# Adding the residual rows: by a load and a VectorE addition, or by a transfer that accumulates into SBUF

## The chip, the cores and the metric

The kernel runs on one core of a Trainium2 chip. A core has five engines with a queue of instructions each: TensorE (PE, matmuls), VectorE (DVE), ScalarE (ACT), GpSimd (POOL) and SyncE (SP, which here begins nearly all transfers between HBM and the on-chip memory SBUF). An engine works its queue in order; an instruction that has to wait, for a semaphore of another engine or of a transfer, holds everything behind it in that queue. The metric is the device time of one execution in microseconds (us), lower is better.

## What is computed

One decoder layer over 4096 rows of width 1024, in float32. The normalised and modulated input feeds three groups of heads (banded attention, RWKV-7, gated linear attention); their gated outputs are joined, go through one output projection, and the result is normalised, gated and added to the input row:

```python
y = jnp.concatenate([attn, rwkv, gla], axis=-1) @ w_out
return x + gate[:, None] * _rmsnorm(y, g_post)
```

The change concerns the last line only, the addition of `x`.

## The kernel before

The rows are cut into 16 tiles of `NT` = 256 rows (`NS` = 16), and each tile into two halves of 128 rows, one row per SBUF partition. A first part (to about 1075 us) prepares the weights and runs the two recurrent groups over all tiles, writing their outputs to a scratch tensor in HBM (`mscr`). A second part runs attention and the output projection, tile by tile: `stage_s` and `stage_v` belong to attention, `stage_m` joins the groups and splits the joined values into pairs of float16 (`mtp`), and `stage_p2` does, for tile i, the output of tile i - 1 (`outp`), the gates (`gates`, matmuls into `gp`) and the queries, keys and values of the next tile (`qkv`, matmuls into `kp`, `qp`, `vp`; the values go through HBM, `vscr`, and come back as `v` in eight loads).

`outp(i)` computes the projection of the tile as seven products (a fast matrix scheme on halves of the operands) into a PSUM bank `op`. Four of the weight blocks stay in SBUF (`o`), three do not and are loaded in turn into one buffer `ov`, each in two halves, as soon as the product that used the buffer has read a half. DVE and ACT combine the products into `yv`, two buffers of 128 rows x 1024 that all tiles but the last share. When a half is complete, `norm` takes the sum of squares (ACT), forms a reciprocal root in a dozen small DVE steps on one column (`sy`, `nwt`, `ry`), scales the half by it and by the gate row `gn` (the DVE instruction `yv<-yv,ry,x`; `gn` lies in the same buffer as the rows of x, so the profile calls both x), adds the rows of x (`yv<-yv,x`) and has SP store it (`out<-yv`). The rows of x come by SP into `xo`, a single buffer of 128 rows: the second half's rows are loaded as soon as the first addition has read it. The last tile is handled apart (`end`, `last_square`, `last_norm`) with its own buffers.

The order of each engine's instructions is neither that of the program text nor one written by hand. Every call passes through a `Lane`, which gives it to a planner (`Order.note`). The planner estimates the duration of each instruction from its size, notes which one reads or writes what another wrote, and in `pin` plays the whole second part through and fixes, per engine, the order that it found. `rank` is the place in the program's text, moved by `urgent` and `lag`. So an edit of a cost, or a removed instruction, can move others.

Of the kernel before, what the change touches and what calls it, by code (L numbers as in the profile page):

```python
# [12 lines left out]
F32 = mybir.dt.float32  # L13
# [3 lines left out]
ALU = mybir.AluOpType  # L17
# [4 lines left out]
P = 128  # L22
D = 1024
# [40 lines left out]
class Order:  # L64
# [34 lines left out]
    def note(self, eng, name, outs, ins, func, r):  # L99

        st = Step()
        st.ins, st.eng, st.table, st.array, st.bytes, st.then = r.ins, str(eng.engine).split(".")[-1], None, None, 0, []
        st.joint = self.joint
        st.half, st.rank = None, len(self.steps) + self.lag
        e, o = st.eng, outs[0]
        on_psum = [a for a in ins if str(a.tensor.space) == "PSUM"]
        n = max(math.prod(a.shape[1:]) for a in [o, *ins[:1]])
        cols = len([a for a in ins[1:] if math.prod(a.shape[1:]) == 1]) if n > 1 else 0
        if e == "PE":
            f32, lhs = ins[0].dtype == F32, self.region(ins[0])  # L110
            n = math.prod(o.shape[1:])
            _, p0, p1, _ = self.region(o)
            rows, cs = (lhs[1] // 32, (lhs[2] + 31) // 32), (p0 // 32, (p1 + 31) // 32)
            rows, cs = [(0, 4) if b - a > 2 else (a, b) for a, b in (rows, cs)]
            mode = (rows[1] - rows[0], cs[1] - cs[0])
            took = n * (2 if f32 else 1) / 2400 + 0.003
            took = max(took, 0.056 if not f32 else 0.0 if mode[1] < 4 else 0.109 if n > 16 else 0.21)
            issue = 0.017 if f32 and mode == (1, 2) else 0.009 if f32 and mode[0] == 1 else 0.007
            cells = [4 * a + b for a in range(*rows) for b in range(*cs)]
            st.array = (mode, cells, 2 if f32 and name == "matmul" else 1, took, issue)  # L120
            st.occ = st.lat = 0.0
        elif e == "SP":
            st.bytes = math.prod(ins[0].shape) * SIZE[ins[0].dtype]
            kb = st.bytes / 1024
            st.occ = 0.47
            st.lat = next((t for k, t in ((8, 1.9), (32, 2.0), (128, 2.3), (256, 2.6), (512, 3.5)) if kb <= k), 4.8)
        elif e == "Activation":
            st.occ = (0.05 if on_psum else 0.093) + 0.093 * (len(ins) - 1) + 0.832e-3 * n
            st.lat = st.occ + 0.1
            if len(outs) > 1:  # L130
                st.occ += 0.187
                st.lat = st.occ + 0.02
            st.table = LN_TABLE if func == AF.Ln else EXP_TABLE if func in (AF.Exp, AF.Tanh) else None
        elif e == "Pool":
            if name == "memset":
                st.occ = 0.06
            elif name == "tensor_copy":
                st.occ = 0.25 if n <= 2 else 0.11 + 0.95e-3 * n
            else:
                st.occ = 0.42 + 1.5e-3 * n if n <= 512 else 1.85e-3 * n  # L140
            st.lat = st.occ + 0.05
        else:
            if name == "tensor_reduce":
                n = math.prod(ins[0].shape[1:])
            fast = name in ("tensor_scalar", "tensor_single_scalar") and not on_psum and o.dtype == F32
            fixed, rate = 0.065 + 0.06 * (cols > 0), 1.04e-3
            if fast:
                rate = 0.53e-3
            elif name == "transpose":
                fixed = 0.09  # L150
            elif name == "memset":
                fixed, rate = 0.05, 0.3e-3
            elif name == "tensor_tensor" and len(o.shape) == 3 and o.shape[2] <= 16 and n > 16:
                fixed, rate = 0.09, 1.55e-3
            st.occ = fixed + rate * n
            st.lat = st.occ + 0.085

        k, st.needs, st.turn = len(self.steps), {}, []
        out_r, in_r = [self.region(a) for a in outs], [self.region(a) for a in ins]
        if e in ("Activation", "DVE"):  # L160

            st.half = (out_r[0][1], in_r[0][1] if e == "Activation" and in_r and out_r[0][2] - out_r[0][1] <= 64 else None)
        tiles = {a.tensor.name: a.tensor for a in [*outs, *ins]}

        if e == "SP" and self.behind is not None:
            st.turn.append(self.behind)

        def need(j, data=False):
            st.needs[j] = st.needs.get(j, False) or data

        for t, tensor in tiles.items():
            if t not in self.known:
                self.known.add(t)
                if t in self.held and tensor.tag:
                    held = self.slots.setdefault((tensor.owner_uid, tensor.tag), [])

                    if held and self.users.get(held[-1]):
                        st.turn.append(self.users[held[-1]][0])
                    if len(held) == self.held[t]:
                        for j in self.users.get(held.pop(0), ()):  # L180
                            need(j)
                    held.append(t)
            elif t in self.held and self.users.get(t):
                st.turn.append(self.users[t][0])
            if str(tensor.space) == "PSUM":
                for j in self.users.get(t, ()):
                    need(j)

        def meet(a, b):
            return a[1] < b[2] and b[1] < a[2] and (a[3] is None or a[3] & b[3])  # L190

        def covered(a, b):
            return b[1] <= a[1] and a[2] <= b[2] and (a[3] is None or not a[3] & ~b[3])

        for a in in_r:
            for w, j in self.wrote.get(a[0], ()):
                if meet(a, w):
                    need(j, True)
        for a in out_r:
            if a[3] is not None:  # L200
                for old in (self.wrote, self.read):
                    for w, j in old.get(a[0], ()):
                        if meet(a, w):
                            need(j)
                    old[a[0]] = [(w, j) for w, j in old.get(a[0], ()) if not covered(w, a)]
            self.wrote.setdefault(a[0], []).append((a, k))
        for a in in_r:
            self.read.setdefault(a[0], []).append((a, k))
        for t in tiles:
            self.users.setdefault(t, []).append(k)  # L210
        st.needs.pop(k, None)
        self.steps.append(st)
# [108 lines left out]
class Lane:  # L321
# [6 lines left out]
    def __getattr__(self, name):  # L328
        f = getattr(self.eng, name)

        def call(*args, **kw):
# [2 lines left out]
            r = f(*args, **kw)  # L334
            self.model.tc.cur_priority += lift
            aps = [a for a in (*args, *kw.values()) if isinstance(a, bass.AP)]
            outs = [aps[0].tensor.name] + ([kw["accum_out"].tensor.name] if kw.get("accum_out") is not None else [])
            accum = kw.get("accum_out")
            self.model.order.behind = self.model.gate if self.model.stage in ("c", "g") else None
# [59 lines left out]
def hybrid_kernel(ctx, tc, x, rows, ada1, adaw, w1, wl, w2, wo, cst, abias, out):  # L399
# [1497 lines left out]
    def outp(i):  # L1897

        f = F[i]
        x2 = xo if i < NS - 1 else t_hT("xo2").rearrange("p a k n -> p (a k n)").bitcast(F32)  # L1900
        SP.dma_start(x2[:, 0:D], x[i * NT + P : (i + 1) * NT, :])
        yield [("m", i)]
        if i == 0:
            yvs = t_A([P, 2, D], "yv")
# [65 lines left out]
        if end:  # L1970
            last_square(f, 1, 0, sums[1])
            last_norm(f, 1, sums[1], x2[:, 0:D])
            SP.dma_start(x2[:, D : 2 * D], x[i * NT : i * NT + P, :])
        else:
            norm(f["oi"], yv[1], x2[:, 0:D], f["blk"][5].rearrange("p a k n -> p (a k n)"),
                 out[i * NT + P : (i + 1) * NT, :])
            SP.dma_start(x2[:, 0:D], x[i * NT : i * NT + P, :])
        yield from full(6)
        add(y12, y12)
        if end:  # L1980
            last_square(f, 0, 1, sums[0])
            last_norm(f, 0, sums[0], x2[:, D : 2 * D])
        else:
            norm(f["oi"], yv[0], x2[:, 0:D], f["blk"][6].rearrange("p a k n -> p (a k n)"), out[i * NT : i * NT + P, :])
        done.add(("o", i))

    def norm(oi, yv, xt, junk, dst):

        sy = st.tile([P, 1], F32, tag="sy", name="sy")
        S.activation(junk, yv, AF.Square, scale=oi, accum_out=sy)  # L1990
# [2 lines left out]
        rsqrt(ry, sy, 1)  # L1993
        V.tensor_mul(ry, ry, oi)
        V.scalar_tensor_tensor(yv, yv, ry, gn, op0=ALU.mult, op1=ALU.mult)
        V.tensor_add(yv, yv, xt)
        SP.dma_start(dst, yv)

    def stage_p2(i):
# [67 lines left out]
    with tc.If(flag == 0):  # L2067
# [42 lines left out]
        with tc.For_i(0, NS, 1) as iv:  # L2110
# [30 lines left out]
            for a in range(2):  # L2141
                xa, oa = [t[:, a].rearrange("o p d -> (o p) d") for t in rows_of]
                SP.dma_start(xo, xa)
                norm(foi, fyv[a], xo, flat[1][:, 0:D], oa)
            G.tensor_copy(fkT[:, :, :, 0:P], fkT[:, :, :, NT : NT + P])
            G.tensor_copy(fv[0], fv[2])
            G.memset(fpm, 0.0)
# [93 lines left out]
```

## Time and profile before

| | |
|---|---|
| Time, median of 3 runs | 2062.37 us (2061.8 to 2066.6) |
| Profiled execution, first to last instruction (its own time) | 2056.7 us |
| TensorE clock granted, mean | 0.986 |
| PE busy | 1950.2 us (95%) |
| DVE busy | 1590.3 us (77%) |
| ACT busy | 1130.8 us (55%) |
| POOL busy | 220.5 us (11%) |
| Addition `yv<-yv,x` | 30 times 1.224 us |
| Load of 128 rows of x (512 KB), from issue to landing | 30 times, median 4.2 us |
| Store `out<-yv` (512 KB) | 30 times, median 2.9 us |

The profile is that of one execution; its times count from the first instruction. A row of a timeline has the start, the time from the first instruction's start to the last one's end, the engine, the line (nearly all are 334, where a `Lane` calls the engine), the operation, output <- inputs with their sizes, and how many were merged; in brackets stands how long the engine had been idle before it, and what ended that. A row of waits has the time in total, how often, and the longest. SPq is SP's queue of transfers: its rows show the issue, and the landing comes later. A row of transfers ends with the median time from issue to landing. A row of a window has its bounds, its length, then the busy time of PE, weight load, DVE, ACT and POOL with the number of instructions, the granted clock, the share of the transfer engines and the rate in GB/s.

### The profile page before, as it was taken

What the parts mean: (1) busy time and instruction counts of PE and PEld (TensorE: products, weight loads), DVE (VectorE), ACT (ScalarE), POOL (GpSimd) and SP (SyncE); (2) the same over time, 40 slices, a digit from 0 to 9 for tenths busy, and PEclk for the clock granted to TensorE, in tenths of its full rate; (3) what the DMA queues carried; (4) which work ended last, traced back from release to release, by engine and by line L of the source; (5) the groups of instructions that cost most, each with busy time, mean ns of one, the idle gap of its engine ahead of it and who ended that gap; (6) DMA issues with size and microseconds to landing.
All of it is one profiled execution on the core that took longest, in us unless ns stands there. A gap on an engine that the chain in (4) does not pass through costs nothing.

```text
span 2056.7 us, 61151 instructions
## 1 busy us (share of the span) xinstructions
PE 1950.2 (95%) x25123; PEld 1517.8 (74%) x25123; DVE 1590.3 (77%) x5120; ACT 1130.8 (55%) x2609; POOL 220.5 (11%) x405
## 2 busy tenths in 40 slices
PE   6899999999999999999898999999999999999997
PEld 3778787778787778887677677777787777777783
DVE  5877877787778986777667887887777877778877
ACT  5867666667767765664334544444444443444543
POOL 1511112321111121111100000000000000000000
PEclk9999999999999999999999999999999999999999
DMA  9433331433413332113433433433334343334314
GB/s 377 139 106 106 106 94 39 145 124 100 142 61 109 124 93 70 60 53 102 134 109 126 153 112 129 127 127 113 110 115 145 115 130 104 119 121 142 111 46 175
DMA packets 151714, 242.06 MB, mean 118 GB/s; under 512 B 48514, under 2 KB 100226, under 8 KB 147204
## 3 DMA queue, kind: packets, MB, share of 16 engines
q1 hardware_dynamic: 151284, 237.56, 35.6%
q8 instruction: 199, 3.26, 0.7%
q14 instruction: 87, 0.71, 0.1%
q10 hardware_dynamic: 144, 0.52, 0.1%
HBM read 177.20 MB, written 60.82 MB: 116 GB/s over the span
## 4 chain that ended last, share of the span: by engine, by line
PE 62%; DVE 21%; ACT 6%; DMA 6%; issue 3%; SPq 2%; DVEq 0%; POOL 0%; ACTq 0%; POOLq 0%
PE gp L334 16%; PE op L334 12%; PE zz L334 6%; PE qp L334 3%; PE lp L334 3%; PE pv L334 3%; PE kp L334 2%; PE gqk L334 2%; PE sc L334 2%; DVE mtp L334 2%; DVE q L334 2%; PE ovp L334 2%; DVE pr L334 2%; SPq L334 2%; DMA xt<-in_x 1%
## 5 line engine op out<-in xcount | busy, mean ns | idle before, releaser
L334 PEld LDWEIGHTS <-mtp 128*128 128x128 f16 x1344 | 130.4, 98 | 141.8 <-issue 4.6
L334 PE MATMUL op<-o,mtp 128*128 128x512 f16 x768 | 172.3, 379 | 0.1
L334 ACT ACTIVATE pr<-pr,nm,lsc 128x256 f32<-128x256 f32 (+1 forms) x256 | 149.2, 585 | 30.9 <-DVE nm L334 30.8
L334 PE MATMUL op<-ov,mtp 128*128 128x512 f16 x576 | 143.1, 379 | 1.3 <-DMA ov<-woscr 0.8
L334 PEld LDWEIGHTS <-hT 128*128 128x128 f16 x1536 | 118.9, 100 | 26.7 <-DVE kg L334 5.3
L334 DVE CUSTOM_DVE_ANT_0 pr<-sc,ab,kept 128x256 f32<-128x256 f32 (+1 forms) x256 | 108.5, 476 | 10.9 <-PE sc L334 10.2
L334 PE MATMUL pv<-gvh,hT 128*128 128x272 f16 x512 | 102.2, 291 | 6.4 <-DVE kg L334 4.5
L334 DVE TENSOR_TENSOR yv<-op,yv 128x512 f32<-128x512 f32 x105 | 70.4, 682 | 47.8 <-PE op L334 33.6
L334 ACT ACTIVATE ag<-gp,gh 128x512 f32<-128x512 f32 x64 | 43.7, 682 | 111.7 <-PE gp L334 111.7
L334 POOL COPY kT<-kT 128x512 f16<-128x512 f16 x15 | 10.2, 682 | 862.0 <-DVE kT L334 862.0
L334 PE MATMUL gqk<-hT,gqkh 128*128 128x256 f16 x512 | 90.3, 276 | 6.0 <-issue 4.2
L334 ACT ACTIVATE mtp<-yv,oi 128x1024 f16<-128x1024 f32 x30 | 34.3, 1144 | 111.8 <-DVE yv L334 111.3
L334 PE MATMUL qp<-hT,q1h 128*128 128x256 f16 x512 | 87.7, 276 | 5.9 <-DVE kT L334 5.9
L334 PE MATMUL lp<-hT,Lh 128*128 128x256 f16 x512 | 92.9, 276 | 0.2 <-ACT vg L334 0.2
L334 PE MATMUL zz<-hT,kh 128*128 128x256 f16 x512 | 92.3, 274 | 0.0
L334 PE MATMUL zz<-hT,vh 128*128 128x256 f16 x512 | 89.1, 275 | 3.4 <-DVE zb L334 3.4
L334 DVE SCALAR_TENSOR_TENSOR ag<-ag,gp 128x512 f32<-128x512 f32 x64 | 43.8, 684 | 62.4 <-ACT ag L334 62.3
L334 PE MATMUL zz<-hT,rh 128*128 128x256 f16 x512 | 91.8, 279 | 0.0
L334 PE MATMUL gp<-hT,q5h 128*128 128x256 f16 x512 | 87.6, 273 | 0.0
L334 PE MATMUL gp<-hT,q3h 128*128 128x256 f16 x512 | 85.5, 273 | 2.0 <-DVE yv L334 1.4
L334 PE MATMUL qp<-hT,q0h 128*128 128x256 f16 x512 | 85.2, 273 | 0.0
L334 PE MATMUL gp<-hT,q4h 128*128 128x256 f16 x512 | 84.9, 273 | 0.0
(460 smaller groups left out, 5981.7 us busy)
## 6 DMA issues: line engine op xcount, KB each, us to landing
ov<-woscr SPq DMA_DIRECT2D x96, 512.0 KB, 4.4
xt<-in_x SPq DMA_DIRECT2D x16, 1024.0 KB, 5.4
hscr<-hT SPq DMA_DIRECT2D x16, 1024.0 KB, 5.0
hT<-hscr SPq DMA_DIRECT2D x16, 1024.0 KB, 4.8
x<-in_x SPq DMA_DIRECT2D x30, 512.0 KB, 4.2
out<-yv SPq DMA_DIRECT2D x30, 512.0 KB, 2.9
cs<-in_w SPq DMA_DIRECT2D x56, 256.0 KB, 3.5
v<-vscr SPq DMA_DIRECT2D x128, 64.0 KB, 3.7
```

What stands on the lines that cost most here:

```text
L334: r = f(*args, **kw)
```

## The change

For the 15 tiles before the last, the rows of x are no longer loaded into a buffer, and DVE no longer adds them. Instead, GpSimd begins a transfer from x in HBM to `yv` in SBUF that adds what it reads to what is there. The store waits for this transfer. The last tile keeps its loads and its additions, and so does the general path at the end of the program (`on_chip=True`), which runs only for other data. The planner learns the new operation: it reads its own destination, and its cost is entered as 1.1 us on GpSimd's queue and 3.0 us more until the data are there.

```diff
@@ cost of an instruction on "Pool" in Order.note
-            if name == "memset":
+            if name == "dma_start":
+                st.occ = 1.1
+            elif name == "memset":
                 st.occ = 0.06
...
-            st.lat = st.occ + 0.05
+            st.lat = st.occ + (3.0 if name == "dma_start" else 0.05)
@@ Lane.call
+            if kw.get("accum_op") is not None:
+                aps.append(aps[0])
@@ outp(i)
-        x2 = xo if i < NS - 1 else t_hT("xo2").rearrange("p a k n -> p (a k n)").bitcast(F32)
-        SP.dma_start(x2[:, 0:D], x[i * NT + P : (i + 1) * NT, :])
+        if i == NS - 1:
+            x2 = t_hT("xo2").rearrange("p a k n -> p (a k n)").bitcast(F32)
+            SP.dma_start(x2[:, 0:D], x[i * NT + P : (i + 1) * NT, :])
...
-            norm(f["oi"], yv[1], x2[:, 0:D], f["blk"][5].rearrange("p a k n -> p (a k n)"),
-                 out[i * NT + P : (i + 1) * NT, :])
-            SP.dma_start(x2[:, 0:D], x[i * NT : i * NT + P, :])
+            rows1 = slice(i * NT + P, (i + 1) * NT)
+            norm(f["oi"], yv[1], x[rows1, :], f["blk"][5].rearrange("p a k n -> p (a k n)"), out[rows1, :])
...
-            norm(f["oi"], yv[0], x2[:, 0:D], f["blk"][6].rearrange("p a k n -> p (a k n)"), out[i * NT : i * NT + P, :])
+            rows0 = slice(i * NT, i * NT + P)
+            norm(f["oi"], yv[0], x[rows0, :], f["blk"][6].rearrange("p a k n -> p (a k n)"), out[rows0, :])
@@ norm
-    def norm(oi, yv, xt, junk, dst):
+    def norm(oi, yv, xt, junk, dst, on_chip=False):
...
-        V.tensor_add(yv, yv, xt)
+        if on_chip:
+            V.tensor_add(yv, yv, xt)
+        else:
+            G.dma_start(out=yv, in_=xt, accum_op=ALU.add)
         SP.dma_start(dst, yv)
```

On SP's queue, the stores of the first output tile and what follows them, before:

```order
L334 DMA out<-yv 128x1024
L334 DMA x_19273<-in_x 128x1024
L334 DMA out<-yv 128x1024
L334 DMA vscr<-vt 128x2x128
L334 DMA x_19273<-in_x 128x1024
L334 DMA ov<-woscr 128x2048 x2
L334 DMA v_19908<-vscr 32x4x128 x4
L334 DMA v_19909<-vscr 32x4x128 x4
```

and with the change:

```order
L336 DMA out<-yv 128x1024 x2
L336 DMA vscr<-vt 128x2x128
L336 DMA ov<-woscr 128x2048
L336 DMA v_19906<-vscr 32x4x128 x4
L336 DMA v_19907<-vscr 32x4x128 x4
L336 DMA ov<-woscr 128x2048 x3
```

The loads of x are gone, and the second half of the weights `ov` moved from ahead of the eight loads of `v` to behind them. In PE's order, two groups of four score matmuls (`sc`) of this tile moved from the second product into the first, and a group of gate matmuls behind the product that they preceded.

On SP's queue at the end of the program, from the last loads of weights to the stores of the last tile (`out<-pr`), before:

```order
L334 DMA ov<-woscr 128x2048 x8
L334 DMA out<-yv 128x1024
L334 DMA x_19273<-in_x 128x1024
L334 DMA ov<-woscr 128x2048 x2
L334 DMA out<-yv 128x1024
L334 DMA out<-pr 128x512 x4
```

and with the change:

```order
L336 DMA ov<-woscr 128x2048 x8
L336 DMA out<-yv 128x1024
L336 DMA ov<-woscr 128x2048
L336 DMA out<-yv 128x1024
L336 DMA ov<-woscr 128x2048
L336 DMA out<-pr 128x512 x4
```

The last two halves of `ov`, which stood together ahead of the second store, now have that store between them. On DVE at the same place, the rows from the split `mtp<-mxe` to the second scaling of `yv`, before:

```order
L334 TENSOR_TENSOR yv<-yv,x_19273 128x1024
L334 SCALAR_TENSOR_TENSOR ry<-nwt,ry 128x1
L334 TENSOR_TENSOR nwt<-ry 128x1
L334 SCALAR_TENSOR_TENSOR nwt<-nwt,sy 128x1
L334 SCALAR_TENSOR_TENSOR mtp<-mxa,msc,mtp 128x512
L334 TENSOR_TENSOR q<-op,q 128x512
L334 SCALAR_TENSOR_TENSOR ry<-nwt,ry 128x1
L334 TENSOR_TENSOR q<-op,q 128x512
L334 TENSOR_TENSOR nwt<-ry 128x1
L334 TENSOR_TENSOR pr<-q,x_19273 128x512
L334 SCALAR_TENSOR_TENSOR nwt<-nwt,sy 128x1
L334 SCALAR_TENSOR_TENSOR mtp<-mxe,msc,mtp 128x512
```

and with the change, from the end of the small steps on:

```order
L336 TENSOR_TENSOR nwt<-ry 128x1
L336 SCALAR_TENSOR_TENSOR nwt<-nwt,sy 128x1
L336 SCALAR_TENSOR_TENSOR ry<-nwt,ry 128x1
L336 TENSOR_TENSOR ry<-ry,oi 128x1
L336 SCALAR_TENSOR_TENSOR yv<-yv,ry,x_19273 128x1024
L336 TENSOR_TENSOR q<-op,q 128x512 x2
L336 SCALAR_TENSOR_TENSOR mtp<-mxa,msc,mtp 128x512
```

The split `mtp<-mxa` and the additions into `q`, which are the last tile's, moved from ahead of the scaling of tile 14's second half to behind it. In the tiles between, no row moves: the additions and the loads are missing, and GpSimd's queue has two transfers ahead of each copy of `kT`.

More of the change, by code (lines that the diff above doesn't have):

```diff
@@ L2143, in hybrid_kernel @@
                 SP.dma_start(xo, xa)
-                norm(foi, fyv[a], xo, flat[1][:, 0:D], oa)
+                norm(foi, fyv[a], xo, flat[1][:, 0:D], oa, on_chip=True)
             G.tensor_copy(fkT[:, :, :, 0:P], fkT[:, :, :, NT : NT + P])
```

## The prediction

> **What bounds the kernel now.** I read the page's first part, then the waits of the matmul engine (PE) over the long stage of 13 equal tiles, then the busy time of one of those tiles, and only then the adding and storing of the finished rows.
>
> ```profile
> PE 1950.2 (95%) x25123; PEld 1517.8 (74%) x25123; DVE 1590.3 (77%) x5120; ACT 1130.8 (55%) x2609; POOL 220.5 (11%) x405
> ...
> PE sc L334 <- DVE m L334: 10.6, 12, 0.9
> ...
> 1262.50:1325.00 62.50, 61.62 (x641) 46.94 (x639) 48.92 (x136) 27.98 (x72) 0.61 (x1) 1.00 0.38 121
> ```
>
> The second row is PE's longest group of waits between 1200 and 2010 us: one wait of 0.9 us per tile, 10.6 us in all, for a score bank that VectorE (DVE) frees. The last row is one tile: PE busy 61.62 of 62.50 us, DVE 48.92, GpSimd (POOL) 0.61. So the stage is PE's. DVE time taken away there is worth something only if it lies ahead of that 0.9 us wait.
>
> ```profile
> 1255.12 1.23 DVE L334 TENSOR_TENSOR yv<-yv,x 128x1024 f32<-128x1024 f32 x1
> 1256.55 0.17 DVE L334 TENSOR_TENSOR sm<-sm,es 128x8 f32<-128x8 f32 x1 [0.20 <-ACT es L334]
> 1265.37 1.29 DVE L334 SCALAR_TENSOR_TENSOR yv<-yv,ry,x 128x1024 f32<-128x1024 f32 x1
> 1267.23 1.22 DVE L334 TENSOR_TENSOR yv<-yv,x 128x1024 f32<-128x1024 f32 x1
> 1270.97 0.69 DVE L334 SCALAR_TENSOR_TENSOR ag<-ag,gp 128x512 f32<-128x512 f32 x1 [1.85 <-ACT ag L334]
> 1293.42 0.60 PE L334 MATMUL sc<-kT,q 128*128 128x256 f16 x4 [0.88 <-DVE m L334]
> ```
>
> It does not. DVE idles for ScalarE (ACT) right after the first addition (0.20 us), and for 1.85 us soon after the second, 22 us ahead of PE's wait. What the additions delay is caught up there.
>
> **The equal tiles.** Removed per tile: two additions of 1.22 us and two loads of x on SP's queue. Added: two transfers begun by GpSimd, and their completion between the scaling of yv and SP's store. Neither addition ended before a wait of PE, so their removal is worth 0. The new cost is L, the time from the end of the scaling (the instruction yv<-yv,ry,x) to the landing of the sum. No row shows an accumulating transfer; the nearest are these, all of 512 KB:
>
> ```profile
> x<-in_x SPq DMA_DIRECT2D x30, 512.0 KB, 4.2
> out<-yv SPq DMA_DIRECT2D x30, 512.0 KB, 2.9
> aw<-in_ada SPq DMA_DIRECT2D x8, 512.0 KB, 11.1
> ```
>
> The floor is the plain load, 4.2: the same rows of x are fetched. Load and store in series make 4.2 + 2.9 = 7.1, since the old yv is also read out of SBUF. The slowest row of this size, 11.1, is my ceiling. I take the middle of 4.2 and 7.1, 5.65, plus one issue of 0.34 as SP's rows show: **L = 6.0**. By the Trainium skill, page "DMA: Bandwidth & Descriptors", section "Anatomy of one DMA — SWDGE (gpsimd) path", a GpSimd transfer takes about 2.0 us + bytes / 436 KB per us, as an estimate 3.2 us here without the read of the destination. By that the two delays below that grow with L would vanish and the kernel would take some 2063; no run here shows it.
>
> What waits for L in an equal tile stands on SP's queue behind the two stores, on POOL's queue behind the two transfers, and in the next writer of yv:
>
> ```profile
> 1268.48 0.34 SPq L334 DMA_DIRECT2D out<-yv  x1
> 1274.05 0.33 SPq L334 DMA_DIRECT2D hT<-hscr  x1
> 1291.35 0.38 SPq L334 DMA_DIRECT2D vscr<-vt  x1
> 1281.50 0.61 POOL L334 COPY kT<-kT 128x512 f16<-128x512 f16 x1 [61.87 <-DVE kT L334]
> 1295.83 0.56 ACT L334 COPY yv<-op 128x512 f32<-128x512 f32 x1
> ```
>
> The second scaling ends at 1265.37 + 1.29 = 1266.7. Its store goes out at 1272.7 instead of 1268.48. The load of hT behind it is for the tile two ahead; vscr, the values that attention needs, goes out at 1291.35, so only L above 24 us would hold it. GpSimd's kT copy has 14 us to spare. ACT's write of yv at 1295.83 comes 20 us after the stores land. So the 13 tiles gain 0 and lose 0, and what hides 26 new landings is the 24 us between the scaling and the next urgent transfer.
>
> **The first tile.** Here the planner's order changes, and the stores stand close ahead of urgent work.
>
> ```profile
> 1164.77 0.34 SPq L334 DMA_DIRECT2D out<-yv  x1
> 1165.15 0.43 SPq L334 DMA_DIRECT2D vscr<-vt  x1
> 1166.57 0.88 SPq L334 DMA_DIRECT2D ov<-woscr  x2
> 1168.10 5.38 SPq L334 DMA_DIRECT2D v<-vscr  x8
> 1159.10 1.27 DVE L334 SCALAR_TENSOR_TENSOR yv<-yv,ry,x 128x1024 f32<-128x1024 f32 x1
> 1169.27 0.60 PE L334 MATMUL sc<-kT,q 128*128 128x256 f16 x4 [0.94 <-DVE m L334]
> 1174.68 2.75 PE L334 MATMUL op<-ov,mtp 128*128 128x512 f16 x12
> 1184.45 0.38 PE L334 MATMUL gp<-hT,q3h 128*128 128x256 f16 x2 [1.40 <-DVE yv L334]
> ov<-woscr SPq DMA_DIRECT2D x96, 512.0 KB, 4.4
> ```
>
> The second scaling ends at 1160.4, and 1.2 earlier without the first addition: 1159.2. With L = 6 its store goes out at 1165.2 and vscr 0.38 later, 1165.6, against 1165.15: +0.45. The second half of the weights ov, until now issued near 1167 ahead of the eight loads of v, now stands behind them: 1168.10 + 0.45 + 5.38 = 1173.9, and with 4.4 us to landing 1178.35. The matmuls that read this half began at 1174.68 + 2.75 / 2 = 1176.0, so PE comes there 2.35 late. The scores moved forward in PE's order wait longer than the 0.94 they waited, but that lies inside this 2.35. Against it, the gate matmuls that waited 1.40 at 1184.45 for DVE now stand behind other products, and I count that wait as gone. Sum **+1.0** at L = 6; +0.5 at 4.2 (vscr then goes as before), +2.1 at 7.1, +6.0 at 11.1. If ov lands in time after all, -1.4 and -0.9 remain: -2.3.
>
> **The end.** The last stores stand between the last two halves of ov on SP's queue, and the last product needs both halves.
>
> ```profile
> 2027.35 1.28 DVE L334 SCALAR_TENSOR_TENSOR yv<-yv,ry,x 128x1024 f32<-128x1024 f32 x1
> 2028.62 0.75 DVE L334 SCALAR_TENSOR_TENSOR mtp<-mxe,msc,mtp 128x512 f16<-128x512 f32 x1
> 2030.60 0.16 DVE L334 TENSOR_TENSOR nwt<-ry 128x1 f32<-128x1 f32 x1
> 2030.80 0.16 DVE L334 SCALAR_TENSOR_TENSOR nwt<-nwt,sy 128x1 f32<-128x1 f32 x1
> 2034.61 1.28 DVE L334 SCALAR_TENSOR_TENSOR yv<-yv,ry,x 128x1024 f32<-128x1024 f32 x1
> 2036.89 0.32 SPq L334 DMA_DIRECT2D ov<-woscr  x1
> 2035.40 1.45 PE L334 MATMUL op<-ov,mtp 128*128 128x512 f16 x6 [0.79 <-DMA ov<-woscr]
> 2041.01 2.75 PE L334 MATMUL op<-ov,mtp 128*128 128x512 f16 x12
> ```
>
> The second scaling now stands ahead of a split (mtp<-mxa) and two additions on DVE. From 2029.4, where the split ahead of it (mtp<-mxe) ends, eight small steps of 0.2 us each from start to start and its own 1.28 bring it to 2032.2. The moved split and additions come later by 0.6 to 2.5 us, which PE's wait for ov until 2035.40 hides. The sum lands at 2032.2 + 6.0 = 2038.2; the store and then ov go out at 2038.2 + 0.38 = 2038.6 instead of 2036.89, and ov lands at 2043.0 (+4.4). The last product's second half wants it at 2041.01 + 2.75 / 2 = 2042.4: **+0.7**. At L up to 5.3 this is 0, at 7.1 +1.8, at 11.1 +5.8. The first half of ov, behind the first store (scaling ended at 2028.6), lands at 2028.6 + 6.0 + 0.4 + 4.4 = 2039.4, in time for 2041.01.
>
> **Sum.** 0 + 1.0 + 0.7 = +1.7 on a profiled span of 2056.7, so 2058.4. The median of the runs, 2062.37, is 5.7 us above that span; I leave this as it is: 2062.4 + 1.7 = **2064.1**.
>
> **Rivals.** (a) *The transfer is slow, L above 8.* First tile and end each grow by 1 us per us of L; from L = 8.2 the two are +3.2 and +2.9, together 0.3% of the kernel, and it is slower. At 11.1 it is 6.0 + 5.8 = +11.8, 2074.2. For it: two reads and a write per row, and GpSimd is held up by DVE, as these rows show:
>
> ```profile
> 1155.36 1.57 POOL L334 COPY kT<-kT 128x512 f16<-128x512 f16 x1 [65.67 <-DVE kT L334]
> 1155.24 1.23 DVE L334 TENSOR_TENSOR yv<-yv,x 128x1024 f32<-128x1024 f32 x1
> 403.27 1.52 DVE L334 TENSOR_TENSOR RA<-zb,ep 128x512 f32<-128x512 f32 x1
> 403.01 1.24 POOL L334 TENSOR_TENSOR gaw<-gaw,scol 128x512 f32<-128x512 f32 x1 [0.81 <-DMA gaw<-in_adaw]
> 1259.69 2.52 DVE L334 STREAM_TRANSPOSE pr<-pr 128x1024 f32<-128x1024 f32 x2
> 1263.42 1.43 PE L334 MATMUL ovp<-pr,v 32*64 32x128 f32 x80
> ```
>
> The copy that takes 0.61 alone took 1.57 beside a DVE addition, 0.96 more. Against it: plain transfers of this size cluster at 2.9 to 4.4. The skill's page "SBUF — State Buffer", section "SBUF: two separate sides", says that a GpSimd-begun DMA starves while DVE runs a 2-port mode, because GpSimd cannot write its descriptors; that would lengthen L by this mechanism, and no run here shows it.
>
> (b) *GpSimd holds DVE.* The other way round: the DVE instruction of 512 columns at 403.27 took 1.52 beside a GpSimd one, where such a one takes 0.69 (the row at 1270.97), 0.83 more. In each equal tile the transposes behind the first transfer end at 1262.2 and PE reads them at 1263.42, so 1.2 us are free. Two such holds, 1.66, would cost 0.46 x 13 = 6.0 on top of the 1.7: 2070.1. Against: one hold per transfer is hidden, and building a transfer touches little data.
>
> (c) *Faster.* If the freed DVE time did reach the 0.9 us wait, up to 10.6 us would go: 2062.4 + 1.7 - 10.6 = 2053.5. The idle stretches above speak against it.
>
> **Chances.** 0.3% of this kernel (6.2 us) is about what a measurement of it can tell from no change. The forecast, L between 4.2 and 8.2 with hidden tiles, 0.68: all of it within 0.3%. (a) 0.21 and (b) 0.06: slower, 0.27 together. (c) 0.05: faster. The range runs from 2059.5 (first tile -2.3, end 0, 0.6 of scatter) to 2075 (L = 11.1 and some scatter).
>
> **What would show it.** From the end of the scaling to the store's issue, 6 us in every tile. The 0.9 us score wait unchanged, a tile of 61.87 + 0.61 = 62.48 us between two kT copies. One new wait of PE for ov near 1176 and one near 2042. SP's x loads gone, DVE's busy time 30 x 1.22 = 37 us less. It is wrong if L is above 8, if the period differs, or if DVE instructions beside GpSimd's transfers grow.

## The result and the profile after

The changed kernel took 2065.24 us against 2059.14 us for the kernel before, medians of 15 runs each, taken beside each other. The ratio is 1.0025, with an interval of 1.0013 to 1.0036: about 5 us slower, at the edge of what can be told from no change, and about three times the +1.7 us that was forecast.

The first rows below are from the page after: busy times, DMA queues (packets, MB, share of 16 engines' time), GpSimd's group of transfers and the DMA issues. The last is PE's wait for scores between 1200 and 2010 us.

```profile
PE 1952.2 (95%) x25123; PEld 1519.3 (74%) x25123; DVE 1556.9 (75%) x5090; ACT 1131.2 (55%) x2609; POOL 242.9 (12%) x435
...
q1 hardware_dynamic: 146964, 221.83, 32.8%
q0 software_dynamic: 4320, 15.73, 4.8%
...
L336 POOL DMA_DIRECT2D yv<-in_x x30 | 26.2, 873 | 746.7 <-DVE yv L336 675.4
...
yv<-in_x POOLq DMA_DIRECT2D x30, 512.0 KB, 5.6
```

```profile
PE sc L336 <- DVE m L336: 10.8, 12, 1.2
```

DVE lost 33.4 us of work and 30 instructions; PE did not notice. Its wait for scores is 10.8 us where it was 10.6. The 30 accumulating transfers took 5.6 us to landing and 0.87 us of GpSimd each.

Where did 5 us come from? A span alone does not say: two profiled executions differ by several us in the first 1090 us, whose instructions both kernels share. So I cut each span at two marks that every run has: GpSimd's copy of kT near 1090 and SP's issue of the last tile's rows of x (xo<-in_x). The first rows of each pair are from the kernel before, the others from the changed one.

```profile
1089.00 0.69 POOL L334 COPY kT<-kT 128x512 f16<-128x512 f16 x1 [37.61 <-DVE kT L334]
2004.07 0.83 SPq L334 DMA_DIRECT2D xo<-in_x  x2
```

```profile
1091.97 0.70 POOL L336 COPY kT<-kT 128x512 f16<-128x512 f16 x1 [38.43 <-DVE kT L336]
2007.03 0.83 SPq L336 DMA_DIRECT2D xo<-in_x  x2
```

The middle, with the first tile and all the equal ones, is 915.07 us before and 915.06 after. The end, from xo to the end of the span, is 2056.7 - 2004.07 = 52.6 before and 2065.3 - 2007.03 = 58.3 after. The whole difference that the change makes lies in the end: +5.6. (The first part, +3.0 here, is scatter: in the ten experiments below the first mark falls anywhere from 1082.1 to 1095.2.)

This is the end after: PE's rows with their waits, then SP's queue, then two steps of the chain of work that ended last, with the time that ov took to land.

```profile
2041.23 1.46 PE L336 MATMUL op<-ov,mtp 128*128 128x512 f16 x6 [3.20 <-DMA ov<-woscr]
2042.52 4.48 PE L336 MATMUL op<-o,mtp 128*128 128x512 f16 x20
2048.53 1.46 PE L336 MATMUL op<-ov,mtp 128*128 128x512 f16 x6 [1.53 <-DVE pr L336]
2050.96 1.46 PE L336 MATMUL op<-ov,mtp 128*128 128x512 f16 x6 [0.97 <-DMA ov<-woscr]
```

```profile
2041.08 0.34 SPq L336 DMA_DIRECT2D out<-yv  x1
2041.51 0.43 SPq L336 DMA_DIRECT2D ov<-woscr  x1
2043.62 0.34 SPq L336 DMA_DIRECT2D out<-yv  x1
2044.05 0.38 SPq L336 DMA_DIRECT2D ov<-woscr  x1
```

```profile
2033.34 7.84 DMA ov<-woscr
...
2044.05 6.87 DMA ov<-woscr
```

The half of the weights ov issued at 2033.34, which no step of the prediction looked at, took 7.84 us to land, and PE waited 3.20 us for it. The last half was issued at 2044.05 behind the second store, took 6.87 us, and PE waited another 0.97 us. In the kernel before, the same two rows of PE read:

```profile
2035.40 1.45 PE L334 MATMUL op<-ov,mtp 128*128 128x512 f16 x6 [0.79 <-DMA ov<-woscr]
2041.01 2.75 PE L334 MATMUL op<-ov,mtp 128*128 128x512 f16 x12
```

There those two halves of ov took 5.4 and 4.8 us to land. (PE's last group of 12 shows as two rows of 6 after, because PE waited between its halves. The wait of 1.53 ahead of it is for DVE, which got its own input late.) What the DMA engines did meanwhile is in the table by stretches (the last two columns are their busy share and the GB/s moved), first before, then after:

```profile
2030.00:2036.00 6.00, 4.74 (x22) 1.98 (x21) 5.75 (x15) 2.34 (x5) 0.00 (x0) 1.00 0.81 283
```

```profile
2036.00:2042.00 6.00, 2.80 (x14) 1.19 (x13) 2.18 (x4) 0.51 (x2) 0.33 (x1) 1.00 1.01 214
```

After, the 16 engines are fully busy and move fewer bytes than before: 214 GB/s at a share of 1.01, against 283 at 0.81.

### The profile page after: what moved, and what is told of

Read it like the earlier page. It is cut to its first block, busy times and chain, and to the rows that moved or that the text cites. A ratio compares the mean times of both kernels' runs of the same rounds, so it can differ in the third digit from the quotient of the medians.

```text
span 2065.3 us, 61139 instructions
## 1 busy us (share of the span) xinstructions
PE 1952.2 (95%) x25123; PEld 1519.3 (74%) x25123; DVE 1556.9 (75%) x5090; ACT 1131.2 (55%) x2609; POOL 242.9 (12%) x435
## 3 DMA queue, kind: packets, MB, share of 16 engines
q0 software_dynamic: 4320, 15.73, 4.8%
## 4 chain that ended last, share of the span: by engine, by line
PE 63%; DVE 21%; DMA 6%; ACT 5%; issue 3%; SPq 2%; DVEq 0%; POOL 0%; ACTq 0%; POOLq 0%
PE gp L336 16%; PE op L336 12%; PE zz L336 7%; PE qp L336 3%; PE lp L336 3%; PE pv L336 3%; PE kp L336 2%; PE sc L336 2%; PE ovp L336 2%; DVE q L336 2%; PE gqk L336 2%; DVE mtp L336 2%; SPq L336 2%; DVE pr L336 2%; PE atp L336 1%
## 5 line engine op out<-in xcount | busy, mean ns | idle before, releaser
L336 PEld LDWEIGHTS <-mtp 128*128 128x128 f16 x1344 | 130.2, 98 | 148.1 <-issue 10.8
L336 POOL DMA_DIRECT2D yv<-in_x x30 | 26.2, 873 | 746.7 <-DVE yv L336 675.4
```

## The experiments

The theory after this reading: the loss lies in the last tile alone, and it comes about because an accumulating transfer takes DMA engine time from the load of ov beside it. The rivals: the loss is only the order on SP's queue (ov behind a store that waits for a sum); it is a fixed cost of a transfer that GpSimd begins; or the equal tiles lose a little each, which two scattered traces hide.

In all of them I read two numbers: the end (from the issue of xo to the end of the span) and PE's waits for ov in it. The table comes from their profiles.

| run | tile 14's rows of x, first half / second half | end, us | longest wait of PE for ov |
|---|---|---|---|
| before | loaded and added / same | 52.6 | 0.8 |
| after | accumulated / accumulated | 58.3 | 3.2 |
| tiles 0-13 accumulate (e1) | loaded / loaded | 52.1 | 0.2 |
| only tile 14 accumulates (e2) | accumulated / accumulated | 56.3 | 2.5 |
| plain transfers (e3) | overwritten / overwritten | 55.7 | 2.9 |
| ov ahead of both stores (e4) | accumulated / accumulated | 56.4 | 2.3 |
| e3 with e4 (e6) | overwritten / overwritten | 53.5 | 0.8 |
| x added twice in tiles 2-12 (e7) | accumulated / accumulated | 57.7 | 3.0 |
| second half only (e8) | loaded / accumulated | 53.0 | 0.6 |
| first half only (e9, and again e11) | accumulated / loaded | 56.9, 57.4 | 2.4, 3.0 |
| first half, half the bytes (e10) | 256 KB accumulated / loaded | 53.6 | 1.1 |

The same code in tile 14 gave 58.3, 57.7 and 56.3 (after, e7, e2), so up to 2 us of the end is scatter, and one smaller difference between two single traces proves nothing.

**Is the loss in the end alone?** e1 keeps the load and the addition in tile 14 and accumulates everywhere else:

```diff
+        loads = i == NS - 2
+        if loads and i < NS - 1:
+            x2 = xo
+            SP.dma_start(x2[:, 0:D], x[i * NT + P : (i + 1) * NT, :])
...
-            norm(f["oi"], yv[1], x[rows1, :], ..., out[rows1, :])
+            norm(f["oi"], yv[1], x2[:, 0:D] if loads else x[rows1, :], ..., out[rows1, :], on_chip=loads)
+            if loads:
+                SP.dma_start(x2[:, 0:D], x[i * NT : i * NT + P, :])
...
```

> Tile 14 alone, the last that uses the shared yv, keeps its loads of x and its VectorE additions; tiles 0 to 13 accumulate. I read the end of the program from the issue of the last tile's two loads into xo to the last instruction: 52.6 us in the kernel before, 58.3 with the change. Theory Q (the accumulating transfers cost time only at the end, where stores and transfers stand in the way of the last weights): the end is 52.6 again, and the time equals that of the kernel before, ratio 1.000. Rival R (a little is lost everywhere, by GpSimd's transfers beside the other work): the end falls, but the ratio stays near 1.0025, since 28 of 30 transfers are still there.

Measured: ratio 0.9995 (0.9982 to 1.0008), the middle 914.8, the end 52.1 us. With 28 of the 30 transfers accumulating the kernel is as fast as before. e2 is its opposite, `loads = i != NS - 2`: one tile accumulates, and that alone has to cost what the change costs.

> The reverse: tiles 0 to 13 keep loads and additions, tile 14 alone accumulates. Theory Q: end at 58.3 us as with the whole change, tiles as before. Rival R: the end at less than 58, since one tile's two transfers make little of the loss.

Measured: end 56.3, 3.7 above before and 2.0 short of the 58.3 that was expected, so by the letter it is the outcome of rival R; 2.0 is also the scatter between equal ends named above. PE's row with the longest wait:

```profile
2035.62 2.72 PE L336 MATMUL op<-ov,mtp 128*128 128x512 f16 x6 [2.52 <-DMA ov<-woscr]
```

What places the loss in the last two of the 30 transfers is e1, where 28 transfers cost nothing. e2 confirms that these two alone cost most of it, at least 3.7 of the 5.6.

**Is it that SP's ov stands behind a late store?** The planner that orders SP's queue takes a GpSimd transfer for 3.0 us. e4 tells it 8.1, about what was measured at the end, and it then issues both halves of ov ahead of both stores:

```diff
-(3.0 if name == "dma_start" else 0.05)
+(8.1 if name == "dma_start" else 0.05)
```

> The change as it is, with one number of the planner changed: the landing of an accumulating transfer is entered 8.1 us after the issue instead of 3.0. The last two halves of ov then stand ahead of both last stores on SP's queue. Theory Q1 (the stores' wait for the sums held the last weights on the queue): end at 52.6 to 54 us, ratio 1.000. Theory Q2 (the accumulating transfers themselves slow the weights' loads, since they read and write SBUF beside reading HBM): the weights still land late, end at 55 us or more, ratio above 1.001.

Measured: ratio 1.0015 (1.0003 to 1.0027), end 56.4. SP's queue is as wanted, and PE waits all the same (queue, then waits):

```profile
2005.29 33.90 SPq L336 DMA_DIRECT2D ov<-woscr  x10
2039.28 1.71 SPq L336 DMA_DIRECT2D out<-yv  x2
```

```profile
PE op L336 <- DMA ov<-woscr: 2.6, 2, 2.3
```

So the order on SP is not all of it: the load of ov itself is slow (7.0 us to landing for the half that PE waited for).

**Is it the accumulation or the transfer?** e3 lets the same transfers write x over yv, in the same places of the queues; the output is then x alone, and the normalised product is left out of it.

```diff
-            G.dma_start(out=yv, in_=xt, accum_op=ALU.add)
+            G.dma_start(out=yv, in_=xt)
```

> The change with plain transfers in the place of the accumulating ones: GpSimd's transfer overwrites yv with the rows of x, so the normalised output is left out of the stored rows; order and waits are those of the change. If the accumulation is what makes a landing long (5.6 us in the tiles, 9.0 and 8.1 at the end), landings fall to about 4.2 in the tiles and 5 to 6 at the end, the transfers' share of the engines per MB halves, and the end comes to 55 or 56 us. If it is only that GpSimd begins them and that they meet the loads of ov, landings stay at 5.5 and the end at 58.

Measured over the whole kernel:

```profile
q0 software_dynamic: 4320, 15.73, 2.4%
...
L336 POOL DMA_DIRECT2D yv<-in_x x30 | 16.1, 535 | 752.1 <-DVE yv L336 680.1
...
yv<-in_x POOLq DMA_DIRECT2D x30, 512.0 KB, 3.9
```

Against the rows after: the same 4320 packets and 15.73 MB take 2.4% of the engines instead of 4.8%, land in 3.9 us instead of 5.6, and hold GpSimd for 0.54 us instead of 0.87. An accumulated byte costs the DMA engines twice the time of a copied one. The end, though, is 55.7, only 2.6 below after, and PE still waits 2.9 us, now for a half of ov that stands behind the second store. e6 joins both edits, plain transfers and 8.1 us in the planner (x alone is stored here too).

> Plain transfers begun by GpSimd (the normalised output is left out of the stored rows) and the planner's 8.1 us, so both suspects are gone: no load of weights stands behind a store at the end, and the transfers use the engines half as long. If the loss at the end is the sum of the two (stores ahead of ov on SP's queue, ov slowed by the accumulation), the end from the issue of xo is 52.6 to 53.3 us, as in the kernel before. If something third is in it (GpSimd's part, the changed order on VectorE), it stays at 55 or above.

Measured: end 53.5, waits of 0.8 and 0.3 us. SP's queue and PE's waits:

```profile
1997.82 32.30 SPq L336 DMA_DIRECT2D ov<-woscr  x10
2030.21 0.86 SPq L336 DMA_DIRECT2D out<-yv  x2
```

```profile
PE op L336 <- DMA ov<-woscr: 1.1, 2, 0.8
```

The four form a square: 58.3 (accumulating, ov behind stores), 56.4 (accumulating, ov ahead), 55.7 (plain, behind), 53.5 (plain, ahead). Copying instead of accumulating is worth 2.6 and 2.9 us, the order 1.9 and 2.2, and with both causes gone 0.9 of the 5.6 stays, a little more than expected. But each corner is one trace, and e4's is not like the others: there alone PE's clock fell behind the wait (see the last section). The 20 matmuls behind it took 6.17 us, and 4.48 in the other three:

```profile
2038.64 6.17 PE L336 MATMUL op<-o,mtp 128*128 128x512 f16 x20
```

Without these 1.7 us e4's end would be 54.7, as an estimate, and the same differences 2.6 and 1.2 for copying, 3.6 and 2.2 for the order. All keep their sign, so that both count is likely; which counts more is open. The changed order on VectorE was not tried alone.

**Which of the two transfers?** e8 accumulates only the second half of tile 14, e9 only the first; the other half is loaded into xo beforehand and added by DVE as before.

```diff
+        late = i == NS - 2
+        if late:
+            x2 = xo
+            SP.dma_start(x2[:, 0:D], x[i * NT + P : i * NT + 2 * P, :])
...
+            norm(f["oi"], yv[1], x2[:, 0:D] if late else x[rows1, :], ..., out[rows1, :], on_chip=late)
```

(e9 has the same for rows 0 to 127 of the tile and yv[0].)

> In tile 14 the first half keeps its load and addition, the second half accumulates; the planner puts both last halves of ov ahead of the second store. Only the load of ov that the accumulation overlaps can suffer. If overlap with one accumulating transfer is enough to make ov late: end at 55 us or more. If it takes two at once, or the queue: 52.6 to 53.5 us.

> The reverse: in tile 14 the first half accumulates, the second keeps its load and addition; the first of the last two halves of ov stands behind the first store. If each transfer costs its part, the end is at 54 to 55.5 us and this and the other half add up to the 5.6 us of the whole change. If it takes both at once, both stay under 53.5 us.

Measured: 53.0 for the second alone, 56.9 for the first alone. The end of e8 shows a sum that takes as long (8.3 us to landing) and hurts little: the last two halves of ov were issued by 2042.02, and the transfer began at 2042.03. The half of ov issued beside it took 6.1 us (3.6 in e1), and PE waited 0.60 us for it:

```profile
2048.21 1.46 PE L336 MATMUL op<-ov,mtp 128*128 128x512 f16 x6 [0.60 <-DMA ov<-woscr]
```

In e9 the transfer began at 2027.66, and ov, issued 1.3 us after it, took 6.6 us to land (GpSimd's row, then PE's):

```profile
2027.66 0.86 POOL L336 DMA_DIRECT2D yv<-in_x  x1 [68.74 <-DVE nwt L336]
```

```profile
2035.62 1.47 PE L336 MATMUL op<-ov,mtp 128*128 128x512 f16 x6 [2.35 <-DMA ov<-woscr]
2036.92 6.60 PE L336 MATMUL op<-o,mtp 128*128 128x512 f16 x22
```

So the first transfer is enough, and it is the one that runs into the load of ov that PE needs next. Here SP's queue ahead of that half is the same as before the change, and no store stands in front of it. Its 56.9 lies above the 54 to 55.5 that was expected if each transfer cost its part. What the second one costs at its place in the changed kernel e8 does not say: there it began 28.4 us after the issue of xo, in e8 32.4 us.

**Bytes or a fixed cost?** e10 is e9 with half the bytes: only columns 0 to 511 of these 128 rows are accumulated, and the other columns go out without x.

```diff
-            G.dma_start(out=yv, in_=xt, accum_op=ALU.add)
+            G.dma_start(out=yv[:, 0 : D // part], in_=xt[:, 0 : D // part], accum_op=ALU.add)
```

> As the run in which only the first half of the last equal tile accumulates, but its transfer adds only columns 0 to 511 of these 128 rows (256 KB of x instead of 512 KB; the other columns keep the normalised output without x). Measured there: 56.9 us from the issue of the pair of x rows to the end of the span, PE waiting 2.35 us for ov; with no accumulating transfer in this tile 52.1. Theory Q2 (the transfer's bytes take the DMA engines' time from the weights ov that are loaded beside it): half the bytes, about half the harm: PE's wait 0.8 to 1.5 us, the end 53.5 to 55.0. Rival (a fixed cost of a transfer begun by GpSimd, or the order of the issues alone, whatever the bytes): wait 2.2 to 2.6, end 56.4 to 57.2.

> The same kernel as in which only the first half of the last equal tile accumulates, once more, to see how far one look scatters. Both theories: end 56.9 and a wait of PE for ov of 2.35, each within 0.5 us. If it differs by more than 1 us, the halved transfer beside it tells nothing by less than that.

Measured: end 53.6 with half the bytes, wait 1.09; the whole transfer once more 57.4, wait 2.98, a little more than the 0.5 us of scatter that was expected. PE's row and SP's half of ov beside the transfer (KB, and us to landing), first e10, then e11:

```profile
2029.73 1.46 PE L336 MATMUL op<-ov,mtp 128*128 128x512 f16 x6 [1.09 <-DMA ov<-woscr]
```

```profile
ov<-woscr SPq DMA_DIRECT2D x1, 512.0 KB, 5.2
```

```profile
2040.08 1.87 PE L336 MATMUL op<-ov,mtp 128*128 128x512 f16 x6 [2.98 <-DMA ov<-woscr]
```

```profile
ov<-woscr SPq DMA_DIRECT2D x1, 512.0 KB, 7.5
```

The half of ov beside the transfer took 6.6 and 7.5 us to land with one accumulating transfer of 512 KB (e9, e11), 7.0 to 8.1 with a second one behind it (e2, e4, after, e7), 5.2 with 256 KB, and 4.5 to 5.9 beside copies alone (e1, e8, before, e3, e6). A fixed cost would have left 56.4 to 57.2. (Of the 3.3 to 3.8 us between the ends about 1 is PE's clock, which fell behind the longer wait; see the last section. The matmuls took 1.7 us longer, but the last half of ov landed only some 1 us before PE came to it. The landings and the waits named here don't depend on the clock.) That the engines' time is what is shared is the reading that fits the halved share in e3 as well.

**Are the equal tiles really free, or just short of a limit?** e7 sends a second accumulating transfer of the same rows in tiles 2 to 12, so x is added twice there.

```diff
             G.dma_start(out=yv, in_=xt, accum_op=ALU.add)
+            if twice:
+                G.dma_start(out=yv, in_=xt, accum_op=ALU.add)
```

> The change, with a second accumulating transfer of the same rows behind the first in tiles 2 to 12 (x is added twice there). The time from the scaling to the store doubles to 11 or 12 us in those tiles. The prediction's step (up to 24 us hide behind the next urgent transfer): 62.48 us from kT copy to kT copy, and 915.1 us from the first kT copy to the issue of xo, both unchanged. Rival: the longer wait on SP's queue or the doubled traffic reaches PE, and the period grows by some tenths.

Measured, two copies of kT that are seven tiles apart, and the transfers:

```profile
1468.07 0.62 POOL L336 COPY kT<-kT 128x512 f16<-128x512 f16 x1 [7.11 <-DVE kT L336]
...
1905.38 0.62 POOL L336 COPY kT<-kT 128x512 f16<-128x512 f16 x1 [6.78 <-DVE kT L336]
```

```profile
yv<-in_x POOLq DMA_DIRECT2D x52, 512.0 KB, 5.7
```

(1905.38 - 1468.07) / 7 = 62.47 us, the same as with one transfer. Its middle is 915.95, 0.9 above after, and all of that lies in the first two intervals of kT (66.95 and 63.81 against 66.38 and 63.43), which end at 1217.90, ahead of the first doubled transfer at 1254.32: scatter. Doubling the change in an equal tile costs nothing.

**A faster version?** None came out. e1, which leaves the collision away, ties with the kernel before, as it must: what it saves is DVE time, and PE bounds the tiles.

## Why the prediction was right and wrong

**The sum came out within 0.3%, as the likeliest case had it; its term for the end was wrong, and the one for the first tile too large.** Forecast: 0 + 1.0 + 0.7 = +1.7. Measured: 5.6 at the end, and -0.2 in the first tile with +0.3 in an early one, in the middle as a whole 0.0. That 2064.1 stands so near 2065.24 is partly luck: the medians beside each other were 2059.14 and 2065.24, while the sum was made on 2062.37, and the two wrong terms, one too small by 4.9 and one too large by 1.2, cancel in part.

**L: right.** The rows after in an equal tile, on DVE, GpSimd and SP:

```profile
1256.56 1.28 DVE L336 SCALAR_TENSOR_TENSOR yv<-yv,ry,x 128x1024 f32<-128x1024 f32 x1
```

```profile
1258.21 0.86 POOL L336 DMA_DIRECT2D yv<-in_x  x1 [35.81 <-DVE yv L336]
```

```profile
1263.99 11.92 SPq L336 DMA_DIRECT2D out<-yv  x2
1276.81 0.34 SPq L336 DMA_DIRECT2D hT<-hscr  x1
```

The scaling ends at 1257.84, the store goes out at 1263.99: L = 6.15 against 6.0. The Trainium skill's rule of 2.0 us + bytes / 436 KB per us (page "DMA: Bandwidth & Descriptors", section "Anatomy of one DMA — SWDGE (gpsimd) path") made 3.2 us of it; measured were 3.9 to landing for a plain transfer (e3) and 5.6 for an accumulating one.

**The equal tiles: right.** A tile is 62.48 us, as forecast, (1909.32 - 1471.97) / 7 between the copies of kT:

```profile
1471.97 0.61 POOL L336 COPY kT<-kT 128x512 f16<-128x512 f16 x1 [13.56 <-DVE kT L336]
...
1909.32 0.61 POOL L336 COPY kT<-kT 128x512 f16<-128x512 f16 x1 [13.58 <-DVE kT L336]
```

Only the interval from 1284.26 to 1347.02 is 0.28 longer, with a score wait of 1.2 in it. DVE's busy time fell by 33.4, not 37. Rival (c), that freed DVE time would reach the score wait, fell with the unchanged wait; rival (b), GpSimd holding DVE, with the unchanged tile, and e7, with twice the transfers, left it unchanged as well.

**The first tile: the mechanism right, the size off, +1.0 forecast and -0.2 measured.** SP's queue after, and PE's wait:

```profile
1168.38 0.43 SPq L336 DMA_DIRECT2D vscr<-vt  x1
1168.90 0.79 SPq L336 DMA_DIRECT2D ov<-woscr  x1
1171.28 4.51 SPq L336 DMA_DIRECT2D v<-vscr  x8
1175.89 3.95 SPq L336 DMA_DIRECT2D ov<-woscr  x2
```

```profile
1179.71 1.46 PE L336 MATMUL op<-ov,mtp 128*128 128x512 f16 x6 [0.23 <-DMA ov<-woscr]
```

With the offset of 2.97 between the two traces, vscr is 0.26 later (0.45 forecast) and ov does stand behind the eight loads of v. But these took 4.51 us instead of 5.38, and ov landed in 3.8 instead of 4.4. It came at 1179.7, by before's clock 1176.7, where 1178.35 was forecast, so PE waited 0.23 us and not 2.35. PE came out of that product 0.76 late, and the gate matmuls' 1.40 is gone, as counted. These two would make -0.6; where the other 0.4 lies was not traced.

**The end: wrong, +0.7 forecast and +5.6 measured.** The step that failed is "lands at 2038.2 ... ov lands at 2043.0 (+4.4)": it took the tile's L and the usual landing of ov into a place where both run at once, and its price followed ov behind the second store only. The second scaling ended at 2033.77 + 1.28 = 2035.05 (2032.1 by before's clock, 2032.2 forecast); its sum was stored at 2043.62, L = 8.6. The first one's L was 9.5 (2031.58 to 2041.08). By before's clock (2.96 less) the delay builds up like this:

- the half of ov that PE needs next is issued 0.47 later and takes 7.84 instead of 5.45 us: PE is 2.9 late;
- the last half then goes out 4.2 later than before: these 2.9, and 1.3 because the second store is ahead of it until 2043.62;
- it takes 6.87 instead of 4.8: 2.1 more, 6.3 in all;
- before, it landed at 2036.89 + 4.8 = 2041.7 and was wanted at 2042.4. Less this 0.7, the second half of PE's last group starts 5.6 late.

The experiments bear out the parts: the 7.84 by e9, e10 and e3, the order by e4 and e6, though not how much each is worth. Rival (a) had named "the transfer is slow" with L above 8. At these two transfers it held, in the other 28 it did not; and its price was put on the stores, while in the list above 4.5 of the 6.3 us are slower loads of ov (2.4 and 2.1).

**DVE starving GpSimd**, the rule of the Trainium skill's page "SBUF — State Buffer", section "SBUF: two separate sides", shows no sign of having made these sums slow. DVE's row behind them:

```profile
2042.72 0.69 DVE L336 TENSOR_TENSOR q<-op,q 128x512 f32<-128x512 f32 x1 [4.54 <-PE op L336]
```

The sums took 9.0 and 8.1 us to landing, until 2041.0 and 2043.6. DVE was idle for the 4.54 us up to 2042.72, and in the stretch of 6 us quoted above (DVE busy for 2.18) the transfer engines had a share of 1.01, so they were not short of work. In the equal tiles, where DVE had much to do, the sums landed in 5.6 us. Beside the first 6 us of the first sum DVE was busy, so a part by that rule is not excluded there.

## What to carry to other kernels

An accumulating transfer is no free addition: here it took the DMA engines twice a copy's time, so ask which load will be under way beside it and who waits for that load. In a long equal stage with 24 us to spare it costs nothing, and takes work off VectorE that is worth nothing when TensorE bounds. At a pipeline's end, where weights arrive just in time, price the collision with the neighbour's landing, not only the transfer's own time, and keep the load and the addition there.

## What the runs showed of the hardware

Two things were not expected. The doubled engine time per byte is the first: 4.8% against 2.4% of 16 engines for the same 15.73 MB, and 7.9% for the 27.27 MB of e7.

The second is a price behind PE's wait. In e2, e4, e7, e9 and e11 the matmuls after a wait of 2.3 to 3.0 us ran slower, in after, after 3.2 us, and in e3, after 2.9 us, they did not. The group of 20 matmuls behind the wait, 4.48 us in after, is in e7:

```profile
2038.39 6.17 PE L336 MATMUL op<-o,mtp 128*128 128x512 f16 x20
```

The stretch of e11 behind its wait shows a granted clock (third number from the right) of 0.70, where the stretches quoted above for before and after have 1.00:

```profile
2042.00:2046.00 4.00, 4.00 (x14) 1.59 (x13) 1.26 (x2) 0.00 (x0) 0.00 (x0) 0.70 0.93 283
```

That is 1.6 to 1.7 us in some runs and none in others; in the changed kernel's own trace a second wait for ov stands there instead. The end pays all of it only where the last half of ov is there in time, as in e4.

The Trainium skill, page "TensorE: Matmul & The Clock Gate", section "Part 1: The HAM clock gate", has the clock drop after at least one idle window of about 3.4 us. Here it dropped after waits of 2.3 to 3.0 us and stayed after one of 3.2, so the length of the wait does not decide alone. What fits is where the wait falls. In all twelve traces the granted clock changes only after whole steps of 3.41 us. In e11 the step from 2037.59 to 2041.00 holds nearly all of the wait: PE is busy for 0.92 us in it, and the next step is granted 0.50. In after the wait is spread over two steps, with 1.41 and 2.22 us of PE, and the clock stays at 1.00. From 1075 us on, each step at full clock in which PE was busy for at most 39% was followed by one at half the clock, and none with 42% or more was. In the first part some busier steps (up to 64%) lost the clock too, so this is no complete rule, and no run was made to try it.
